# Context gates moved between the recurrence features, with twelve latent gates of the last layer beside them

## The chip, the cores and the metric

The kernel runs on one core of one Trainium2 chip. The metric is the device time in microseconds (us) from the first to the last instruction of the program on that core. TensorE (PE in the rows) does the matrix products into PSUM, VectorE (DVE) and ScalarE (ACT) do elementwise work, GpSimd (POOL) does elementwise work and gathers, and SyncE (SP) issues most DMAs. Each engine works through its own list of instructions in the order in which the program was built, so an instruction that waits also holds whatever stands behind it.

## The reference, cut to what matters

Two layers transform 512 latent and 256 context tokens of width 1024. In each layer one input projection feeds four token mixers and four vectors of gates:

```
p_lat = (x * (1 + sc1) + sh1) @ w_in[l]
p_ctx = (ctx * (1 + csc1) + csh1) @ w_in[l]
mla_lat, rwkv_lat, gqa_lat, win_lat, gate_lat = split_last(p_lat, GROUP_WIDTHS)
...
acc = gates[:, :, 0] * (ys[0] @ w_branch[0])      # gates = sigmoid(gate_pre), 4 x 1024 columns
```

The gates are needed only when the branches are merged, late in a layer. The context stream is not carried out of the last layer, so its context gates are never needed; its latent gates are. Gates are 4096 columns, made in 32 chunks of 128.

## The kernel before, in words

Every product with a weight is done in three passes to keep fp32 accuracy. `wload` and `wtile` fetch a weight chunk of 512 KB on SP's queue (`wr`), round it on ScalarE (`wH`, line 204), and subtract on VectorE or GpSimd to get the rest (`wL`, line 205, called a split below). TensorE then does, for each of eight slices of the inner dimension, high by high, high by low and low by high: 24 matmuls for a chunk, of 256 columns for the context tokens and 512 for the latent ones. Four pairs of buffers hold split weights in stage S1.

A layer goes through these stages:

- S1, features. `feature(f, m)` makes 15 chunks of the recurrence projection for all 768 tokens (48 matmuls each: 24 of 512, 24 of 256 columns). For each of four pairs of heads the order is `k`, `r`, `v`; after them `rates` (small products, line 349), `keys` (products `kksq`, line 360, on the normalised keys), `unit` (transposes `krep` and the scaling of `kkr`), and `prepare`, a long run on VectorE and ScalarE. `prepare` of one pair is done while TensorE makes the features of the next; its last result `ksum` feeds the product in `bonus` (line 430).
- S1, natural. `natural` makes three blocks of columns in token order (line 499), with two or three rounds of `ada_round` (modulation weights of 8 MB each) between them.
- S1, heads. `heads(0)` and `heads(1)` normalise, rotate, transpose and split queries and keys. `context` makes the 32 context gates in layer 0, sixteen behind each `heads`; in the last layer it makes none.
- S2. The recurrence for four pairs of heads, one after the other. For each pair VectorE inverts blocks by `eliminate` (lines 742 and 745), then twelve steps go from engine to engine. Thirty-two latent gates (`gate_lat`, split on GpSimd) have the lowest priority, and the scheduler puts their matmuls wherever it sees TensorE free.
- Then attention and merge, the output projection, and the experts.

The builder's scheduler sets the order of every engine from the order of the calls and its own view of what is ready. The names in rows: `pw` is a two-bank PSUM tile of S1 or S2, `pl` the PSUM tile of a latent gate or of an ada round, `pn` that of a natural block or of a small product, `X` the modulated input.

Of the kernel before, what the change touches and what calls it, by code (L numbers as in the profile page):

```python
# [8 lines left out]
F32 = mybir.dt.float32  # L9
# [47 lines left out]
STEPS = 3  # L57

# [20 lines left out]
def tile_backbone(ctx: ExitStack, tc: tile.TileContext, I, out, taps=None, upto=99):  # L79
# [89 lines left out]
    def mm_acc(outs, lhs, rhs, nk):  # L169
        """outs: list of (psum ap, lo, hi); lhs/rhs: functions k -> (H, L); moving sliced by lo:hi"""  # L170
# [13 lines left out]
    # ------------------------------------------------------------------ weight stream  # L184
# [26 lines left out]
    # ------------------------------------------------------------------ modulation  # L211
# [3 lines left out]
    def ada_round(l, r, ps, sb, ring=None, bufs=4):  # L215
        """columns r * 2048 .. of layer l: four groups of 512, one column tile of the array each"""
# [30 lines left out]
    def xtiles(l):  # L247
        """the modulated input of layer l in two parts, latent and context, on the other side of SBUF"""
# [7 lines left out]
    # ------------------------------------------------------------------ layers  # L256
    for l in range(DEPTH):
# [5 lines left out]
        with xlat:  # L263
            # ---------------------------------------------------------- S1 projections
            T3B = 12
            with xctx, ExitStack() as e1:
# [42 lines left out]
                # RWKV features, transposed  # L309
                with ExitStack() as er:  # L310
                    pr = er.enter_context(tp(name=f"pr{l}", bufs=1))
                    psw = er.enter_context(tp(name=f"s0w{l}", bufs=3, space=PSUM))
# [74 lines left out]
                    def prepare(hp, r, k, v, kk, rt):  # L387
                        """decayed queries and keys of a pair of heads, bonus"""
# [63 lines left out]
                    for hp in range(4):  # L452
                        r, k, v = [pr.tile([P, T], F32, name=nm(n), tag="rk", bufs=8) for n in "rkv"]
                        feature(4 + hp, k)
                        feature(hp, r)
                        rt = [rates(hp, 0)]
                        kk, pn = keys(hp, k)
                        for f in late:
                            f()
                        feature(8 + hp, v)  # L460
# [8 lines left out]
                    for f in late:  # L469
                        f()  # L470
                if upto < 2:
                    return
# [11 lines left out]
                # natural projections  # L484
# [22 lines left out]
                def rope(dst, x, b, nh, hd):  # L507
                    """dst, x: [P, nh, hd]"""
# [80 lines left out]
                # context gates  # L589
                def gate_chunk(f, lat, cx, pp, dst):  # L590
                    W = wload(I["w_gate"][l, f], [P, DC, P])
                    pw = pp.tile([P, 1024], F32, name="pw")
                    proj_t(pw, W, lat, cx)
                    lo, hi = (0 if lat else TL), (T if cx else TL)
                    ac.activation(dst[:, lo:hi], pw[:, lo:hi], AF.Tanh, scale=0.5)
                    ac.dma_start(gscr[f][:, lo:hi], dst[:, lo:hi])
# [1384 lines left out]
```

## Time and profile before

| what | us |
|---|---|
| median of three runs | 6534.53 |
| lowest and highest of them | 6518.1 and 6548.82 |
| span of the profiled execution (the page gives no other time for it) | 6533.5 |
| layer 0: features, natural, heads with gates, S2 | 217.0, 175.6, 146.1, 526.3 |
| layer 1: features, natural, heads, S2 | 210.0, 174.0, 37.9, 507.9 |

The stages are stretches of the span, cut where the first instruction of the next one starts on TensorE. The rest of the span is attention, the experts and the norms, which the change does not touch. The profile's page gives busy time per engine; a busy TensorE may still be working at half its clock, so the granted clock (PEclk, as a share of 2.4 GHz) is read beside it.

### The profile page before, as it was taken

What the parts mean: (1) busy time and instruction counts of PE and PEld (TensorE: products, weight loads), DVE (VectorE), ACT (ScalarE), POOL (GpSimd) and SP (SyncE); (2) the same over time, 40 slices, a digit from 0 to 9 for tenths busy, and PEclk for the clock granted to TensorE, in tenths of its full rate; (3) what the DMA queues carried; (4) which work ended last, traced back from release to release, by engine and by line L of the source; (5) the groups of instructions that cost most, each with busy time, mean ns of one, the idle gap of its engine ahead of it and who ended that gap; (6) DMA issues with size and microseconds to landing.
All of it is one profiled execution on the core that took longest, in us unless ns stands there. A gap on an engine that the chain in (4) does not pass through costs nothing.

```text
span 6533.5 us, 95628 instructions
## 1 busy us (share of the span) xinstructions
PE 5912.4 (90%) x35605; PEld 4895.5 (75%) x35605; DVE 4508.9 (69%) x9402; ACT 2371.0 (36%) x4585; POOL 2217.2 (34%) x1721
## 2 busy tenths in 40 slices
PE   8898998999897998889899788798999888999998
PEld 5677665778776886667677566666678788999998
DVE  6535554667698857888888674546456798578887
ACT  3223222444335842222222332222334467433333
POOL 1101222000038846656655211133100168444442
PEclk9998897999998999999999899799899999999999
DMA  4455222031435688888899435422121446888896
GB/s 175 157 192 181 84 85 72 11 87 58 148 109 185 229 280 305 303 305 315 316 334 335 171 107 177 131 93 74 68 64 41 156 148 226 291 292 294 296 331 246
DMA packets 532162, 1220.90 MB, mean 187 GB/s; under 512 B 46321, under 2 KB 249201, under 8 KB 524017
## 3 DMA queue, kind: packets, MB, share of 16 engines
q1 hardware_dynamic: 339728, 718.16, 33.2%
q0 software_dynamic: 111168, 406.63, 17.0%
q10 hardware_dynamic: 80800, 90.00, 4.0%
q8 instruction: 281, 4.60, 0.3%
q14 instruction: 185, 1.51, 0.1%
HBM read 1041.41 MB, written 173.21 MB: 186 GB/s over the span
## 4 chain that ended last, share of the span: by engine, by line
PE 48%; DVE 14%; issue 8%; DMA 8%; POOL 5%; ACT 2%; SPq 0%; ACTq 0%; POOLq 0%; DVEq 0%
PE pu L1538 10%; PE pa L1789 7%; PE po L1101 4%; POOL row L1008 3%; PE pl L176 3%; PE pm L176 3%; DMA row<-in_peer_v,gix 3%; PE pw L1070 3%; PE ptp L182 2%; PE pv L1789 2%; PE pn L499 2%; DMA row<-in_peer_v 2%; PE pg L1465 2%; DMA row<-in_peer_u,gix 2%; PE pw L176 1%
## 5 line engine op out<-in xcount | busy, mean ns | idle before, releaser
L1538 PE MATMUL pu<-HX,wH 128*128 128x512 f32 (+2 forms) x4608 | 1327.4, 371 | 11.5 <-ACT wH L1524 6.0
L1538 PEld LDWEIGHTS pu<-HX,wH 128*128 128x128 f32 x4608 | 855.9, 194 | 115.1 <-ACT ga L1777 7.0
L1538 PE MATMUL pu<-HX,wL 128*128 128x512 f32 (+2 forms) x2304 | 848.3, 368 | 41.6 <-POOL wL L1526 36.1
L1008 POOL DMA_INDIRECT row<-in_peer_u,gix x384 | 495.3, 1290 | 513.9 <-DVE row L1648 281.1
L1008 POOL DMA_INDIRECT row<-in_peer_v,gix x384 | 495.5, 1290 | 454.6 <-DVE accn L1657 237.9
L1630 ACT CAST wH<-row 128x1024 fp32r<-128x1024 f32 x384 | 401.9, 1047 | 609.2 <-DMA row<-in_peer_v 286.6
L1789 PE MATMUL pa<-CL,wH 128*128 128x512 f32 (+1 forms) x1536 | 566.5, 369 | 26.0 <-DVE CL L1769 25.8
L1789 PE MATMUL pa<-CH,wH 128*128 128x512 f32 (+1 forms) x1536 | 563.7, 367 | 21.5 <-ACT CH L1764 21.4
L1648 DVE SCALAR_TENSOR_TENSOR row<-row,hn 128x1024 f32<-128x1024 f32 x384 | 504.4, 1323 | 99.0 <-DMA row<-in_peer_u,gix 96.8
L1789 PE MATMUL pa<-CH,wL 128*128 128x512 f32 (+1 forms) x1536 | 562.3, 366 | 0.0
L1657 DVE SCALAR_TENSOR_TENSOR accn<-row,gcw,accn 128x1024 f32<-128x1024 f32 x381 | 519.3, 1374 | 61.4 <-DMA row<-in_peer_v,gix 60.8
L1646 DVE TENSOR_TENSOR wL<-row,wH 128x1024 fp32r<-128x1024 f32 x384 | 478.3, 1246 | 119.4 <-ACT wH L1630 118.6
L1538 PEld LDWEIGHTS pu<-HX,wL 128*128 128x128 f32 x2304 | 445.4, 193 | 100.9 <-POOL wL L1526 42.7
L204 ACT CAST wH<-wr 128x1024 fp32r<-128x1024 f32 (+1 forms) x222 | 231.0, 1043 | 574.9 <-PE pl L176 188.4
L980 POOL TENSOR_TENSOR lnst<-lnst,mhalf 128x4 f32<-128x4 f32 (+3 forms) x8 | 9.4, 1180 | 1183.1 <-DVE lnst L979 1183.1
L176 PE MATMUL pl<-X,wH 128*128 128x512 f32 x1024 | 403.7, 457 | 3.7 <-DVE qk L585 3.2
L205 POOL TENSOR_TENSOR wL<-wr,wH 128x1024 fp32r<-128x1024 f32 x64 | 214.4, 3355 | 545.4 <-ACT wH L204 278.2
L1449 POOL TENSOR_SCALAR B<-cst,T 128x128 f32<-128x128 f32 x330 | 383.4, 1170 | 33.6 <-PE pg L1465 20.7
L1789 PEld LDWEIGHTS pa<-CL,wH 128*128 128x128 f32 x1536 | 291.2, 190 | 72.2 <-DVE CL L1769 41.3
L1789 PEld LDWEIGHTS pa<-CH,wH 128*128 128x128 f32 x1536 | 291.2, 190 | 61.4 <-ACT CH L1764 29.1
L205 DVE TENSOR_TENSOR wL<-wr,wH 128x1024 fp32r<-128x1024 f32 (+1 forms) x158 | 191.3, 1213 | 189.3 <-ACT wH L204 188.1
L1764 ACT CAST CH<-ga 128x512 fp32r<-128x512 f32 (+1 forms) x256 | 145.0, 566 | 467.6 <-DVE ga L1761 349.3
(400 smaller groups left out, 13619.4 us busy)
## 6 DMA issues: line engine op xcount, KB each, us to landing
row<-in_peer_v SPq DMA_DIRECT2D x256, 512.0 KB
wr<-in_uT SPq DMA_DIRECT2D x128, 512.0 KB
row<-in_uT SPq DMA_DIRECT2D x128, 512.0 KB
wr<-in_ada_w SPq DMA_DIRECT2D x96, 512.0 KB
wr<-in_w_gate SPq DMA_DIRECT2D x96, 512.0 KB
gdr<-gall SPq DMA_DIRECT2D x32, 1024.0 KB
Gt<-gdr SPq DMA_DIRECT2D x32, 1024.0 KB
gdr<-big SPq DMA_DIRECT2D x24, 1024.0 KB
```

Source lines behind the costliest of these rows:

```text
L176: pe.matmul(o, lw, rw[:, lo:hi], start=(k == 0 and a == 0), stop=(k == nk - 1 and a == 2))
L204: ac.copy(H, raw)
L205: lsplit[0] = (split or ve).tensor_tensor(L, raw, H.bitcast(F32), op=OP.subtract)
L1008: gp.indirect_dma_start(out=rows, out_offset=None, in_=tab, in_offset=bass.IndirectOffsetOnAxis(ap=ix, axis=0))
L1101: pe.matmul(o[r0:r0 + 64, o0:o0 + P], vx(kb), pt[:, j * P:(j + 1) * P], start=(j == 0), stop=(j == nk - 1))
L1449: (gp if e == "gp" else ve).tensor_scalar(B[:, j, :], iota, T3[:, 1, t_ + j:t_ + j + 1], T3[:, 2, t_ + j:t_ + j + 1], op0=OP.is_equal, op1 ...
L1538: pe.matmul(pw[:, :hi - lo], w[:, k, :], x[:, k, :], start=(k == 0 and i == 0), stop=(k == DC - 1 and i == 2))
L1630: ac.copy(H, ready[nx[1]])
L1646: ve.tensor_tensor(L, raw, H.bitcast(F32), op=OP.subtract)
L1648: ve.scalar_tensor_tensor(raw, raw, 1.0, hn[y], op0=OP.mult, op1=OP.mult, accum_out=acts[y][:, j:j + 1])
L1657: ve.scalar_tensor_tensor(accn[y], raw, gcw[y][:, j:j + 1], accn[y], op0=OP.mult, op1=OP.add)
L1789: pe.matmul(pv[:, :TD], w[:, ds], x, start=(k == 0 and i == 0 and (fresh or s == 0)), stop=(k == 1 and i == 2 and (fresh or s == NS - 1)))
```

## The change

The context gates are made by a new function `gate_early` in the features stage, two behind each `k`, each `r` and each `rates`/`keys` block of the four pairs in layer 0 (24), and the remaining eight behind the last feature. In the last layer, which has no context gates, one latent gate is made at each of these twelve places, and `gate_lat` in S2 starts from number 12. `psw` of the features stage shrinks from three two-bank tiles to two, and the two banks go to a pool of two single tiles, `psg`. Nothing is computed differently. Docstrings and comments were dropped as well, which shifts line numbers.

```diff
+EARLYG = (32, 12)
...
+                def gate_early(f, pp):
+
+                    H, L = wload(I["w_gate"][l, f], [P, DC, P])
+                    lo, hi = (0, TL) if last else (TL, T)
+                    x = X[0 if last else 1]
+                    pw = pp.tile([P, 512], F32, name="pg")
+                    mm_acc([(pw[:, :hi - lo], 0, hi - lo)], lambda k: (H[:, k, :], L[:, k, :]),
+                           lambda k: (x[0][:, k, :], x[1][:, k, :]), DC)
+                    g = s1.tile([P, T], F32, name=nm("gate"), tag="t3", bufs=T3B)[:, :hi - lo]
+                    ac.activation(g, pw[:, :hi - lo], AF.Tanh, scale=0.5)
+                    ac.dma_start(gscr[f][:, lo:hi], g)
+
+                early = list(range(EARLYG[l]))
+
+                def gates(n, pp):
+                    for _ in range(min(n, len(early))):
+                        gate_early(early.pop(0), pp)
...
-                    psw = er.enter_context(tp(name=f"s0w{l}", bufs=3, space=PSUM))
+                    psw = er.enter_context(tp(name=f"s0w{l}", bufs=2, space=PSUM))
+                    psg = er.enter_context(tp(name=f"s0g{l}", bufs=2, space=PSUM))
...
                         feature(4 + hp, k)
+                        gates(2 - last, psg)
                         feature(hp, r)
+                        gates(2 - last, psg)
                         rt = [rates(hp, 0)]
                         kk, pn = keys(hp, k)
                         for f in late:
                             f()
+                        gates(2 - last, psg)
                         feature(8 + hp, v)
...
                     for f in late:
                         f()
+                    gates(len(early), psg)
...
                 heads(0, nats[1])
-                context(0, 16)
+                ada()
                 heads(1, nats[2])
-                context(16, 32)
+                ada()
...
-                for f in range(32):
+                for f in range(EARLYG[l] if last else 0, 32):
                     gate_lat(f)
```

TensorE, layer 0, between the second and the third pair of the features stage. `la` feeds the rates, `v` is transposed for the pair before, `kksq` is this pair's norm, `ksum` the bonus of the pair before. Before, these small products stand together ahead of the `v` feature, and `kksq` stands 27 matmuls into it:

```order
L349 MATMUL pw<-la,a_289 128x512
L349 MATMUL pw<-la,a_289 128x256
L182 MATMUL pw<-cst,v_433 128x128 x6
L430 MATMUL pw<-ksum_678,cst 128x512
L430 MATMUL pw<-ksum_678,cst 128x256
L302 MATMUL pw<-X_112,wH_915 128x512
L306 MATMUL pw<-X_114,wH_915 128x256
```

The same place in the change, where `pg` is the PSUM tile of an early gate:

```order
L177 MATMUL pg<-X_115,wH_1185 128x256
L177 MATMUL pg<-X_114,wL_1186 128x256
L369 MATMUL pw<-la,a_292 128x512
L369 MATMUL pw<-la,a_292 128x256
L183 MATMUL pw<-cst,v_436 128x128 x6
L177 MATMUL pg<-X_114,wH_1258 128x256
L380 MATMUL pn<-cst,kksq_1229 128x2 x6
L177 MATMUL pg<-X_115,wH_1258 128x256
L177 MATMUL pg<-X_114,wL_1259 128x256
```

Forty-eight gate matmuls now stand ahead of these products, `kksq` has moved ahead of the bonus and of the whole `v` feature, and 47 more gate matmuls stand around the bonus behind it. On VectorE the stretch from one pair's `krep` to the next pair's `kkr` holds two splits before and five in layer 0 (four in layer 1) now; three more stand in one row ahead of the next `krep`.

TensorE, layer 0, at `heads(1)`. Before, the twenty transposes of `xo` and ten of `nwin` have context gates on both sides (gate matmuls are L306 here):

```order
L306 MATMUL pw<-X_115,wH_4000 128x256
L306 MATMUL pw<-X_114,wL_4001 128x256
L182 MATMUL pw<-cst,xo_4032 128x128 x5
L182 MATMUL pw<-cst,xo_4045 128x128 x5
L182 MATMUL pw<-cst,xo_4064 128x128 x5
L182 MATMUL pw<-cst,xo_4083 128x128 x5
L182 MATMUL pw<-cst,nwin 128x128 x10
L306 MATMUL pw<-X_114,wH_4135 128x256
```

In the change the ada round (L225, `glat` its result) ends just ahead of them, and the first latent gate of S2 (`pl<-X`) follows:

```order
L225 MATMUL pl<-wr_4426,sc_104 32x512 x2
L183 MATMUL pl<-cst,glat_4430 128x128 x4
L183 MATMUL pw<-cst,xo_4580 128x128 x5
L183 MATMUL pw<-cst,xo_4593 128x128 x5
L183 MATMUL pw<-cst,xo_4612 128x128 x5
L183 MATMUL pw<-cst,xo_4631 128x128 x5
L183 MATMUL pw<-cst,nwin 128x128 x10
L177 MATMUL pl<-X_112,wH_8461 128x512
```

Nothing but transposes is left to TensorE between the end of the ada round and S2.

TensorE, layer 1, S2, the last recurrence step but one of the fourth pair. Before, it holds a gate matmul (L176) between the product of `S` with `AR` (L836) and that with `TT` (L844):

```order
L836 MATMUL pw_37608<-S_37601,AR_36343 64x64 x2
L836 MATMUL pw_37608<-S_37601,AR_36346 64x64 x2
L176 MATMUL pl<-X_30567,wL_38764 128x512
L807 MATMUL pw_37660<-S_37601,AR_36343 64x64
L844 MATMUL pc<-w0s_37613,TT 64x64 x4
```

The same step in the change:

```order
L843 MATMUL pw_37987<-S_37980,AR_36759 64x64 x2
L843 MATMUL pw_37987<-S_37980,AR_36762 64x64 x2
L814 MATMUL pw_38039<-S_37980,AR_36759 64x64
L851 MATMUL pc<-w0s_37992,TT 64x64 x4
L864 MATMUL pw_37987<-UV_36767,nat_37890 64x64 x2
```

The gate matmul is gone. Most steps hold four to seven gate matmuls before; in the change they still do in the first two pairs, while the third and fourth pair's steps, the whole inversion of the fourth pair, and that of the third pair behind its 77th gate matmul hold none. At the end of layer 1's features stage, 61 matmuls of the first natural block now stand ahead of the last bonus, where before all of them stood behind it; in layer 0 the 144 matmuls of six gates stand there instead, behind the bonus.

## Rows read from the trace of the kernel before

**Rows 1.** The page: busy time of each engine, share of the span, instructions.
```profile
PE 5912.4 (90%) x35605; PEld 4895.5 (75%) x35605; DVE 4508.9 (69%) x9402; ACT 2371.0 (36%) x4585; POOL 2217.2 (34%) x1721
```

**Rows 2.** Windows by stage; columns: stretch, length, busy time (instructions), PEclk, DMA share, GB/s.
```profile
35.00:252.00 217.00, 178.41 (x895) 141.88 (x896) 174.54 (x247) 77.89 (x113) 36.99 (x61) 0.89 0.37 126
427.60:573.70 146.10, 120.77 (x884) 103.34 (x880) 65.22 (x75) 50.23 (x75) 4.64 (x2) 0.92 0.75 240
3735.00:3945.00 210.00, 174.33 (x884) 139.38 (x884) 158.12 (x217) 69.80 (x97) 38.05 (x46) 0.88 0.34 114
4118.97:4156.90 37.93, 13.82 (x63) 10.38 (x61) 30.29 (x45) 8.31 (x12) 2.13 (x1) 0.59 0.72 209
4156.90:4664.80 507.90, 458.20 (x4012) 330.96 (x4012) 286.13 (x718) 131.25 (x285) 148.72 (x124) 0.88 0.28 90
```

**Rows 3.** Waits of TensorE, layer 0 features: total us, times, longest.
```profile
PE pw L430 <- DVE ksum L427: 20.2, 3, 16.8
PE pw L349 <- ACT buf L336: 6.1, 3, 2.2
```

**Rows 4.** Timeline of VectorE, layer 0 features: start, length, instruction, idle before.
```profile
131.76 1.23 DVE L205 TENSOR_TENSOR wL<-wr,wH 128x1024 fp32r<-128x1024 f32 x1 [4.27 <-ACT wH L204]
133.43 0.56 DVE L368 COPY krep<-kst 128x768 f32<-128x768 f32 x1
...
167.88 0.61 DVE L355 TENSOR_SCALAR kkr<-k,vec 128x768 f32<-128x768 f32 x1
...
177.90 0.56 DVE L368 COPY krep<-kst 128x768 f32<-128x768 f32 x1
```

**Rows 5.** Timeline of TensorE, layer 1 features; 93 feature matmuls stand between these two.
```profile
3827.80 0.82 PE L182 MATMUL pn<-cst,krep 128*128 128x128 f32 x6
...
3844.61 1.55 PE L349 MATMUL pw<-lw,w 64*128 64x512 f32 x4
```

**Rows 6.** Timeline of ScalarE: results of context gates; one more gate ends between them.
```profile
558.86 0.39 ACT L595 ACTIVATE gate<-pw 128x256 f32<-128x256 f32 x1 [0.40 <-ACT gate L595]
564.83 0.39 ACT L595 ACTIVATE gate<-pw 128x256 f32<-128x256 f32 x1 [0.40 <-ACT gate L595]
```

**Rows 7.** Timeline of ScalarE in S2, layer 1: results of two successive latent gates.
```profile
4435.43 0.59 ACT L911 ACTIVATE glat<-pl 128x512 f32<-128x512 f32 x1
4441.03 0.58 ACT L911 ACTIVATE glat<-pl 128x512 f32<-128x512 f32 x1
```

**Rows 8.** Window during layer 0's last ada round, columns as in rows 2.
```profile
440.00:460.00 20.00, 15.20 (x76) 7.42 (x76) 6.32 (x8) 3.58 (x5) 0.00 (x0) 0.92 1.08 364
```

**Rows 9.** Timeline of VectorE, layer 1: heads(1) begins.
```profile
4138.37 0.81 DVE L514 TENSOR_TENSOR rope<-nwin,cst 128x640 f32<-128x640 f32 x1
```

**Rows 10.** Timeline of TensorE, layer 1: first natural block, three matmuls apart.
```profile
3949.13 0.55 PE L499 MATMUL pn<-wH,X 128*128 128x416 f32 x2
...
3949.71 0.55 PE L499 MATMUL pn<-wH,X 128*128 128x416 f32 x2
```

**Rows 11.** Timeline of VectorE, layer 1, inversion of the last pair.
```profile
4570.53 0.48 DVE L742 TENSOR_TENSOR tmp<-W,X 128x150 f32<-128x150 f32 x2
4570.91 4.80 DVE L745 TENSOR_TENSOR X<-X,tmp 128x150 f32<-128x150 f32 x2
...
4582.60 2.29 DVE L742 TENSOR_TENSOR tmp<-W,X 128x50 f32<-128x50 f32 x1
```

**Rows 12.** Timeline of GpSimd in the same stretch.
```profile
4563.42 12.19 POOL L205 TENSOR_TENSOR wL<-wr,wH 128x1024 fp32r<-128x1024 f32 x2 [3.13 <-ACT wH L204]
```

**Rows 13.** Timeline of TensorE, one recurrence step of the third pair, layer 1.
```profile
4520.21 0.34 PE L836 MATMUL pw<-S,AR 64*64 64x64 f32 x8
...
4524.39 0.73 PE L176 MATMUL pl<-X,wH 128*128 128x512 f32 x2
4525.05 0.34 PE L836 MATMUL pw<-S,AR 64*64 64x64 f32 x8
```

**Rows 14.** Window at the start of layer 1's first recurrence.
```profile
4220.00:4240.00 20.00, 20.00 (x191) 15.26 (x191) 8.19 (x9) 6.04 (x12) 4.33 (x5) 0.50 0.02 4
```

More of the change, by code (lines that the diff above doesn't have):

```diff
@@ L587, in heads @@
                                 ac.dma_start(qkscr[br][i][:, :, (b - 1) * P:b * P], qk[i].bitcast(F32))
[L590 to L596, printed above, removed]
-                rounds = ROUNDS[l][:]
-                def context(a, b):
-                    for f in range(a, b):
-                        if not last:
-                            g = s1.tile([P, T], F32, name=nm("gate"), tag="t3", bufs=T3B)
-                            gate_chunk(f, False, True, psw, g)
-                        if f % 16 == 8:
-                            ada()
+                rounds = ROUNDS[l][:]
                 def ada():
```

## The prediction

> **What bounds the kernel now.** I read the page first: TensorE is busy for 90% of the span [rows 1], so work that only changes its place gains nothing; what counts is the time in which TensorE waits, at the place that work leaves and at the place to which it goes. Then I cut the span into the stages that the change touches [rows 2]. In layer 0's features TensorE is idle for 217.0 - 178.4 = 38.6 us, in layer 1's for 210.0 - 174.3 = 35.7, each time with VectorE busy for 75 to 80%. In layer 0's heads, with the 32 context gates, it is idle for 25.3. Layer 1's heads show what that stage is without gates: 37.9 us, of which VectorE works 30.3. S2 of layer 1, with 32 latent gates, takes 507.9 us at 458.2 of TensorE. Last I went into single places: the waits of TensorE in the features [rows 3], where the longest, 16.8 us, is the last bonus waiting for `ksum`, and the timelines of one pair.
>
> One pair of the features is a circle of 177.90 - 133.43 = 44.5 us from `krep` to `krep` [rows 4]. From `krep` to the end of the next `kkr` (167.88 + 0.61) are 35.1 us, in which VectorE has no gap; the other 9.4 are the norm, the rest of the `v` feature and small products. So VectorE sets the first stretch and TensorE the second, and a matmul is free only if it is put into the first.
>
> **The change part by part.** *The price of a gate.* Two context gates end 564.83 - 558.86 = 5.97 us apart [rows 6], so one is 3.0 us of TensorE, or 0.125 a matmul; 32 are 96. A latent gate takes 5.6 us [rows 7], 0.23 a matmul; twelve are 67. A split on VectorE takes 1.23 us [rows 4]. A feature matmul takes (3844.61 - 3828.62) / 93 = 0.172 us on the mean [rows 5].
>
> *Layer 0's heads, -106.* The 146.1 us lose their gates and become layer 1's bare stretch of 37.9 [rows 2]. The last ada round now has nothing to cover its loads: twelve loads of 0.52 MB, at the 364 GB/s of [rows 8], are 17 us, and behind it `heads(1)` takes 4156.9 - 4138.37 = 18.5 [rows 9]; together 36 to 38 if the loads run at that rate. I take 40. If they ran at half of it, the stage would be 55, so the gain lies between 91 and 108.
>
> *Layer 0's features, +81.* The first pair has TensorE as its limit and pays in full for its six gates: +18. In the three pairs after it the order puts into the first stretch two splits become five, so VectorE needs 35.1 + 3 x 1.23 = 38.8, less the bonus product (under 1 us) that left it: 38. TensorE's own work there is 95 feature matmuls (16.3), about 94 gate matmuls (11.8) and some 5 us of small products, 33 in all: covered. The second stretch gets 47 gate matmuls (5.9), the bonus (some 1.5) and the 27 matmuls of `v` (4.6) that stood ahead of `kksq`: 9.4 + 12.0 = 21.4. The circle is then 59.4 instead of 44.5, and three of them cost +45, where 54 were put in. At the end, 45 gate matmuls stand inside the 16.8 us of waiting and are free; the splits ahead of `ksum` and six gates behind the bonus cost +18. In all 81 of 96. If every idle microsecond were filled it would be 96 - 38 = 58, and if none were, 96.
>
> *Layer 1's features, +40.* The first pair pays three gates, +17. Then the first stretch has two splits more: 35.1 + 2.5, about 37.5, against 33 of TensorE. The second gets 23 latent gate matmuls (5.3) and the 27 of `v` (4.6): 19.3. The circle is 56.8 or, with the bonus product gone from the first stretch, 56.3, three times +11.8: +35. At the end the 61 natural matmuls that now stand ahead of the bonus take 0.193 us each [rows 10], so 11.8 of the last wait is filled: -12. Bounds as before: 31 to 67.
>
> *Layer 1's S2, -30.* Twelve gates leave, all from the third pair's inversion on. The inversion is VectorE's: while GpSimd makes two splits in 12.2 us [rows 12], two subtractions that take 0.48 together as the product ahead of them does cost 4.80; a single one costs 2.29 where its neighbours take 0.22 [rows 11]. So four splits cost the inversion 8.6 us, and the third pair loses one of its own, 2.1: 10.7. The Trainium skill, page SBUF — State Buffer, section "SBUF: two separate sides", says that VectorE and GpSimd hold a port pair for a whole instruction while the loser stands still; the trace agrees (4.80 for 0.48). The rule also speaks against the early splits, which read two operands on VectorE: in layer 0 they could hold GpSimd for 32 x 1.23 = 39 us more, beside 37.0 us of work in 217.0 [rows 2]; by the rule the sum would stay as it is unless `prepare` waits for GpSimd just then, and no row here prices that. Between inversion and recurrence 18 gate matmuls stood in each pair, mostly on the path: -6 for two pairs. A recurrence step takes 4.84 us and holds five or six gate matmuls [rows 13]; two of them stand between the outputs and the next `S` by `AR`, the rest in waits that remain. I take 0.6 us for each of 22 steps: -13. Bounds: 0 if the chain keeps its pace, -67 if TensorE alone set it.
>
> *The smaller pool of `pw`.* Two tiles instead of three make a small product wait for the copy two tiles back; one such wait of 2.2 us stands in every pair already [rows 3]. In layer 0 gate matmuls lie between, in layer 1 two or three only, inside the stretch that VectorE sets. Price nothing, up to 2 us a pair, 12 in all, if that cover is gone.
>
> *The sum.* -106 + 81 + 40 - 30 = -15 on a span of 6533.5. That span lies 1 us under the median of the three runs, so I forecast 6519 us, from 6495 to 6543 by itself (heads 15 worse; features and S2 10 to 15 either way).
>
> **The rivals.** *S2 gives the gates back in full.* If TensorE's queue alone set the pace of the third and fourth pair, S2 would fall by 67 instead of 30: 6482. For it speak 458 us busy of 508 [rows 2]; against it that the inversion is VectorE's.
>
> *VectorE stands at the splits (slower).* A split waits for ScalarE's cast, which waits for one of four buffers that TensorE must have freed; 4.27 us of it show in the pair of [rows 4], and everything of `prepare` is queued behind, then `ksum`, then TensorE's bonus. If each added split of the first stretch (three, and two in layer 1) waits that long, three pairs cost 38 and 26 us more: 6519 + 64 = 6583. It decides when these waits pass 15 us over the six pairs, 2.5 us a pair. Against it: the new order holds buffers for shorter chunks, so they come free sooner.
>
> *The clock.* With no gates beside it the fourth pair's inversion leaves TensorE nearly without work, and its recurrence then starts at 1.2 GHz, as layer 1's first one did, granted 0.50 behind an inversion [rows 14]. If the two bare recurrences ran at that level throughout, the 3.7 us of a step that are not gates would double, +2.6 in 16 steps with outputs, and the 13 gained are gone: 6519 + 41 + 13 = 6573. The Trainium skill, page TensorE: Matmul & The Clock Gate, section "HAM oscillation — how this bites in real kernels", says that a TensorE left waiting falls to half its clock again and again; the row agrees for a start, but no run here shows a whole recurrence without gates.
>
> *The idle only moves.* If the features fill nothing, +96 and +67 stand against -106 and -30: +27, 6562. For it speaks that TensorE's waits are for VectorE, which gets more to do; against it that those 16.8 us at the end are plainly open to work.
>
> **How the numbers follow.** Forecast 0.46; S2 in full 0.21; splits 0.15; clock 0.06; idle only moves 0.12. About half a percent, 33 us, is what a measurement of this kernel can tell. Faster than 6502: all of the second case and a fifth of the first, 0.30. Slower than 6567: two thirds of the splits, most of the clock, a few hundredths of the last, 0.17. Within: 0.53. The range leaves a tenth on either side: 6474 to 6577.
>
> **What would show it.** In the changed profile: layer 0 from the end of the natural blocks to S2's first gate near 40 us; a pair's circle near 59 us in layer 0 and 56 in layer 1, with a wait of TensorE at `kksq` of 4 to 6 us in place of those at `la` and `v`; the inversion of layer 1's fourth pair free of stretched subtractions; its steps near 4.2 us. I am wrong if the circle stays under 54 or passes 64, if layer 0's bare heads take over 50 us, or if bare steps take as long as before.

## The result, and the profile after

The changed kernel is slower: median 6581.42 us against 6534.53, ratio 1.0062 with a 95% interval of 1.0039 to 1.0084, or 41 us (25 to 55). The forecast was 6519, the range ended at 6577. The profiled execution has a span of 6586.8 us, 53.3 more than before.

The same stretches as in [rows 2], cut where the first TensorE instruction of the next stage starts; the natural blocks are shown too:

```profile
core 0: us, PE busy (x) PEld busy (x) DVE busy (x) ACT busy (x) POOL busy (x), PEclk, DMA share, GB/s
35.00:341.00 306.00, 274.01 (x1667) 237.24 (x1665) 212.05 (x278) 118.38 (x174) 45.60 (x61) 0.92 0.49 159
341.00:526.90 185.90, 174.17 (x1177) 141.51 (x1176) 48.50 (x107) 35.06 (x70) 16.70 (x4) 0.95 0.47 154
526.90:575.80 48.90, 28.29 (x116) 12.00 (x112) 30.31 (x46) 8.89 (x13) 0.26 (x1) 0.76 0.87 289
575.80:1118.60 542.80, 489.42 (x4250) 353.57 (x4250) 289.47 (x733) 135.38 (x300) 154.99 (x123) 0.87 0.28 86
3748.00:4015.00 267.00, 254.08 (x1234) 205.07 (x1234) 173.36 (x229) 87.56 (x121) 40.72 (x49) 0.95 0.38 125
4015.00:4182.80 167.80, 157.60 (x1100) 126.78 (x1099) 46.92 (x106) 33.04 (x68) 14.75 (x4) 0.99 0.48 159
4182.80:4220.80 38.00, 14.13 (x63) 10.52 (x61) 30.29 (x45) 8.31 (x12) 2.19 (x1) 0.56 0.73 208
4220.80:4716.80 496.00, 408.91 (x3724) 301.04 (x3724) 272.65 (x718) 112.64 (x261) 113.50 (x112) 0.74 0.23 73
```

Stage by stage, against the table of the profile before:

| stage | before | after | difference | forecast |
|---|---|---|---|---|
| layer 0, features | 217.0 | 306.0 | +89.0 | +81 |
| layer 0, natural | 175.6 | 185.9 | +10.3 | 0 |
| layer 0, heads | 146.1 | 48.9 | -97.2 | -106 |
| layer 0, S2 | 526.3 | 542.8 | +16.5 | 0 |
| layer 1, features and natural | 384.0 | 434.8 | +50.8 | +40 |
| layer 1, heads | 37.9 | 38.0 | 0 | 0 |
| layer 1, S2 | 507.9 | 496.0 | -11.9 | -30 |

The rest of the span is 4 us shorter. Of the 68 us between this span and the forecast's -15, layer 0's features and natural blocks have 18, its heads 9, its S2 16.5, layer 1's features and natural blocks 11 and its S2 18. Two lines stand out. The natural blocks and S2 of layer 0 grew although none of their work changed; and S2 of layer 1, which lost twelve gates of 5.6 us, gave back 11.9 us at a mean granted clock of 0.74 where it had 0.88.

Where it shows, first in VectorE's timeline of one pair in layer 0, the rows that answer to [rows 4]:

```profile
111.48 0.55 DVE L388 COPY krep<-kst 128x768 f32<-128x768 f32 x1
149.39 0.62 DVE L375 TENSOR_SCALAR kkr<-k,vec 128x768 f32<-128x768 f32 x1
170.28 0.56 DVE L388 COPY krep<-kst 128x768 f32<-128x768 f32 x1
```

The circle is 58.8 us, 38.5 to the end of `kkr` and 20.3 behind it. The forecast was 59.4, 38 and 21.4.

Then TensorE's timeline from layer 0's last bonus to the natural blocks:

```profile
317.37 2.90 PE L450 MATMUL pw<-ksum,cst 128*128 128x512 f32 x4 [14.06 <-DVE ksum L447]
...
340.00 1.04 PE L225 MATMUL pl<-wr,sc 128*32 128x512 f32 x2
340.97 0.65 PE L523 MATMUL pn<-wH,X 128*128 128x416 f32 x2
...
350.47 1.06 PE L523 MATMUL pn<-wH,X 128*128 128x416 f32 x2 [6.96 <-ACT wH L205]
```

The wait for `ksum` is still 14.06 us (16.8 in [rows 3]): most gates of the stage's end stand behind the bonus, not in the wait. Then come 20 us of gates, and then a new wait: a cast of `w_in` is late. In the timelines of ScalarE's and SP's queues and the DMA view of 326 to 352 us (busy share in tenths and rate in 40 slices of 0.65 us; an issue's KB and us to landing), what it waits for:

```profile
329.70 0.48 ACTq L505 DMA_DIRECT2D gains<-in_gqa_q_norm  x1
...
333.75 0.38 SPq L196 DMA_DIRECT2D wr<-in_w_in  x1
347.80 0.33 SPq L196 DMA_DIRECT2D wr<-in_ada_w  x1
```

```profile
DMA  9036999989997697612100000000012288899989
GB/s 361 21 36 95 353 388 414 359 239 348 364 363 259 184 260 228 225 75 72 40 23 20 13 22 20 23 19 12 21 30 82 101 247 326 308 243 296 338 276 397
...
gains<-in_gqa_q_norm ACTq DMA_DIRECT2D x1, 256.0 KB, 18.1
```

The load of `w_in` issued at 333.75 lands 15.7 us later, the longest of that tile's here; their median is 5.4. From 339.0 to 345.5, well inside its wait, the DMA moves only 12 to 30 GB/s: the gain vectors of the head norms are loaded in small packets (1526 of the packets in these 26 us are under 512 B), and take 18 us. The DMA engines' busy share is 0 or 1 tenth there, so they are not full either; why a load waits beside them no run shows. The kernel before loads these vectors at the same place, but had `w_in` in SBUF by then. The 7 us of waiting cost more than themselves, since TensorE then goes on at half its clock (window of the next 10 us, columns as above):

```profile
350.00:360.00 10.00, 8.20 (x20) 6.29 (x21) 2.05 (x2) 2.89 (x8) 0.00 (x0) 0.50 0.65 202
```

Last, windows of layer 1's third and fourth recurrence from the first to the last `w0s`, and two steps in VectorE's timeline of the fourth:

```profile
4544.50:4595.00 50.50, 43.56 (x366) 30.74 (x366) 12.26 (x47) 9.06 (x33) 7.72 (x18) 0.50 0.08 25
4658.20:4708.70 50.50, 43.63 (x366) 30.76 (x366) 12.34 (x46) 9.11 (x34) 7.72 (x18) 0.50 0.00 1
```

```profile
4681.02 0.29 DVE L846 TENSOR_TENSOR w0s<-pw,KV 128x128 f32<-128x128 f32 x1 [2.53 <-PE pw L843]
4686.82 0.29 DVE L846 TENSOR_TENSOR w0s<-pw,KV 128x128 f32<-128x128 f32 x1 [2.52 <-PE pw L843]
```

And the same two windows of the kernel before, not shown ahead:

```profile
4489.70:4535.50 45.80, 45.80 (x426) 29.93 (x426) 12.32 (x47) 13.46 (x39) 14.69 (x21) 0.98 0.26 79
4611.10:4656.70 45.60, 44.72 (x422) 29.25 (x422) 14.84 (x49) 13.74 (x40) 10.91 (x19) 0.98 0.15 49
```

With 60 and 56 matmuls fewer, both recurrences take 5 us more. The granted clock is 0.50 from end to end, 1.2 GHz, and TensorE is busy for 86% of the stretch with the step's own small matmuls. The step shown, one with outputs, takes 5.80 us, where [rows 13] has 4.84 with its gate matmuls in it.

### The profile page after: what moved, and what is told of

It reads as the page before. It is cut to its first block, busy times and chain, and to the rows that moved or that the text cites. A ratio compares the mean times of both kernels' runs of the same rounds, so it can differ in the third digit from the quotient of the medians.

```text
span 6586.8 us, 95630 instructions
## 1 busy us (share of the span) xinstructions
PE 5947.9 (90%) x35605; PEld 4929.4 (75%) x35605; DVE 4505.0 (68%) x9414; ACT 2369.7 (36%) x4585; POOL 2195.9 (33%) x1709
## 5 line engine op out<-in xcount | busy, mean ns | idle before, releaser
L1796 PE MATMUL pa<-CH,wH 128*128 128x512 f32 (+1 forms) x1536 | 565.5, 368 | 22.2 <-ACT CH L1771 22.2
L206 DVE TENSOR_TENSOR wL<-wr,wH 128x1024 fp32r<-128x1024 f32 (+1 forms) x170 | 205.8, 1213 | 235.9 <-ACT wH L205 234.4
L177 PE MATMUL pl<-X,wH 128*128 128x512 f32 x832 | 331.4, 461 | 6.1 <-DVE qk L609 6.1
L1796 PEld LDWEIGHTS pa<-CH,wL 128*128 128x128 f32 x1536 | 292.6, 191 | 31.0
```

The costliest lines, as they stand in the source:

```text
L177: pe.matmul(o, lw, rw[:, lo:hi], start=(k == 0 and a == 0), stop=(k == nk - 1 and a == 2))
L206: lsplit[0] = (split or ve).tensor_tensor(L, raw, H.bitcast(F32), op=OP.subtract)
L1796: pe.matmul(pv[:, :TD], w[:, ds], x, start=(k == 0 and i == 0 and (fresh or s == 0)), stop=(k == 1 and i == 2 and (fresh or s == NS - 1)))
```

## The experiments

**Which layer loses it.** Two kernels make one layer's move alone. Each is the changed kernel with one number of its table at zero, and the layer whose gates stay keeps three tiles of `pw`. Where layer 0's gates stay, they are back in the heads, behind the ada rounds.

```diff
-EARLYG = (32, 12)
+EARLYG = (32, 0)     # layer 0 alone
+EARLYG = (0, 12)     # layer 1 alone
...
```

> Only layer 0's 32 context gates move; layer 1's latent gates stay in S2. Theory: in the profile of the changed kernel layer 0's features and natural blocks grew by 99 us and its heads shrank by 97, so the move is worth nothing by itself, and the 17 us that its S2 lost besides, all in one recurrence at granted 0.50, are the clock's and need not come again: 6536 us, up to 6553 if that recurrence is slow here too. Rival (my forecast was right for layer 0 and layer 1 lost it all): 6534 - 25 = 6509.

> Only layer 1's twelve latent gates move; layer 0's context gates stay in its heads. Theory: layer 1's features and natural blocks lose 51 us, its S2 gives back 12, since its last two recurrences run at 1.2 GHz with steps of 5.05 us: 6534 + 39 = 6573. Rival (the forecast for layer 1, +40 and -30, was right and layer 0 lost it all): 6544.

Layer 0 alone: 6544.76 us, ratio 1.0014 (0.9991 to 1.0036), 9 us over the kernel before, the interval from -6 to +24. Its circles are 58.2 us, and all four recurrences of its layer 0 run at granted 1.00. Layer 1 alone: 6571.7 us, ratio 1.0043 (1.0027 to 1.0060), 28 us over (18 to 39). Its circles are 56.4 to 57.9, its last two recurrences 50.4 and 50.5 us at granted 0.50. So the forecast of -25 for layer 0 is outside its interval, and so is +10 for layer 1; the theory's +2 and +39 are inside, the second at the edge. Both layers missed.

**The smaller pool.** The kernel before, with one number changed:

```diff
-psw = er.enter_context(tp(name=f"s0w{l}", bufs=3, space=PSUM))
+psw = er.enter_context(tp(name=f"s0w{l}", bufs=2, space=PSUM))
```

> No gate moves; only the pool of pw in the features has two tiles instead of three. Theory: the third tile was never needed, circles stay at 44.5 and 43.5 us: 6534. Rival (two tiles make every pair wait): up to 2 us a pair, 16 in all, 6550, and the circles 46 us.

```profile
144.33 0.56 DVE L368 COPY krep<-kst 128x768 f32<-128x768 f32 x1
192.03 0.55 DVE L368 COPY krep<-kst 128x768 f32<-128x768 f32 x1
```

These two rows of VectorE's timeline are 47.7 us apart, 3.2 more than in [rows 4]; layer 1's circles are 47.2 to 47.8 instead of 43.6 to 44.5. So the rival holds for the circles, and with more than its 2 us a pair: in layer 0's three circles TensorE waits 23.6 us, six times, for the copies that empty `pw`. The time, 6551.62 us, ratio 1.0013 (0.9997 to 1.0030), fits both: the natural blocks catch up with part of it.

**Is it in the changed kernel's circles?** Two kernels give `pw` its third tile again while layer 0's gates come early (layer 1's don't). In one the gates take their turn in that pool; the other starts from the kernel with eight gates back in the heads (below) and leaves one bank each to the gates and the norm.

```diff
 # share3
-gates(2 - last, psg)
+gates(2 - last, psw)     # psw: bufs=3, no psg
 # banks311
-psw bufs=2, psg bufs=2, psn bufs=2
+psw bufs=3, psg bufs=1, psn bufs=1
```

> Layer 0's 32 gates early, layer 1's not, and no PSUM banks of their own: the early gates take their turn in the pool of pw, which has its three tiles again. Theory: two tiles alone made a circle 47.7 us instead of 44.5, 3.2 more, and the same 3.2 are in the 58.2 of layer 0 alone: circles of 55 us, the kernel 10 to 13 us under layer 0 alone, 6533. Rival (with gates between the features the small products no longer wait for the third tile): circles stay at 58, 6545.

> Layer 0 alone with eight gates back in the heads; in the features the pool of pw has three tiles again, and the early gates and the norm's sums one bank each instead of two. Theory (the 3.2 us a circle that two tiles of pw cost without gates are in the 58.2 too): circles 55 us, the kernel 10 to 13 us under 6522. Rival (they are hidden under the gates, and a single bank makes a gate wait for the tanh of the one before): circles 58 us or more, 6522 or more.

In neither is the circle shorter. With the shared pool the circles are 61.0 to 61.5 us (ratio 1.0031, 1.0013 to 1.0048), longer even than the rival had it. With one bank each they are 58.9 to 60.3 (6519.83 us, ratio 0.9983, 0.9968 to 0.9998). Each of the two takes banks from something else, so neither is a clean test of the third tile. What bears on it more directly is TensorE's waits in the changed kernel's three circles: none is for a copy that empties `pw`, and nearly all, 12.7 us, are for the `tanh` of a gate. So the forecast's price of nothing fits this kernel, by its stated cover.

**Who sets the first stretch.** Layer 0 alone, the early gates' splits on GpSimd:

```diff
-H, L = wload(I["w_gate"][l, f], [P, DC, P])
+wn[0] += 1
+H, L = wtile(I["w_gate"][l, f], [P, DC, P], (wp, w1)[wn[0] % 2], split=gp)
```

> Layer 0's 32 gates early, layer 1's not, and the splits of the early gates on GpSimd instead of VectorE (2.4 us each there, 1.23 on VectorE). Theory (VectorE sets the first stretch, so three added splits are in the circle): first stretch 34.5 to 35 us instead of 38.1, circle 54.5 to 55, the kernel 11 us under layer 0 alone, 6534. Rival (GpSimd's splits make VectorE's two-operand work wait, as they did in the inversion, and prepare's own GpSimd work stands behind them): first stretch 40 us or more, circle over 60, 6550 or more.

The groups of VectorE's work in one first stretch, by form, with busy time and mean ns of one; layer 0 alone and then this kernel:

```profile
L363 DVE SCALAR_TENSOR_TENSOR mixt<-buf,vec,mixt 128x770 f32<-128x770 f32 x3 | 3.1, 1017 | 0.0
L432 DVE SCALAR_TENSOR_TENSOR b<-ta,kkr 128x768 f32<-128x768 f32 x2 | 1.9, 955 | 0.0
```

```profile
L433 DVE SCALAR_TENSOR_TENSOR b<-ta,kkr 128x768 f32<-128x768 f32 x2 | 5.7, 2856 | 0.0
L364 DVE SCALAR_TENSOR_TENSOR mixt<-buf,vec,mixt 128x770 f32<-128x770 f32 x3 | 5.2, 1726 | 0.0
```

The rival: the first stretch is 42.6 to 42.7 us instead of 38.1, the circle 62.8 to 63.9; 6558.09 us, ratio 1.0026 (1.0006 to 1.0046). VectorE has one split in the stretch instead of five and is busy just as long (37.4 and 37.6 us), since two-operand work beside GpSimd's splits takes up to three times as long (2.86 us for 0.96; in the other two stretches of layer 0 alone the mean of these `b` rows is 1.78 already). The Trainium skill, page SBUF — State Buffer, section "SBUF: two separate sides", says that the two engines hold a shared port pair for a whole instruction; these rows agree. And it waits 4.6 us for `pcm`. The splits belong on VectorE here, though it sets the stretch.

**The natural blocks' start.** Layer 0 alone with 24 early gates, the eight of the stage's end back in the heads:

```diff
 for f in late:
     f()
-gates(len(early), psg)
```

> Layer 0 alone with 24 gates early and the eight of the stage's end back in the heads, layer 1's latent gates not early. Theory: the 10 us that the natural blocks lost at their start (loads of w_in and ada_w share two raw buffers and stood behind the eight gates) do not come, nor the 22 us between ksum and the first natural matmul; eight gates cost the heads 24 us, of which up to 10 hide the loads of the last ada round: the first inversion of S2 begins at 582 to 592 us instead of 595, the kernel 3 to 13 us under layer 0 alone, 6532 to 6542. Rival (the natural blocks wait for the loads of w_in whoever is in front): their first copies still come 30 us or more behind ksum, and the kernel is 10 us over layer 0 alone.

TensorE's timeline behind the last `ksum`:

```profile
311.13 2.90 PE L454 MATMUL pw<-ksum,cst 128*128 128x512 f32 x4 [5.14 <-DVE ksum L451]
313.46 0.91 PE L527 MATMUL pn<-wH,X 128*128 128x416 f32 x1
```

The theory, in its numbers: natural matmuls follow the bonus at once, some stand ahead of it already (the wait for `ksum` is 5.14 us instead of 14.1), no wait for `w_in` is left, and S2's first inversion begins at 585.1. 6522.16 us, ratio 0.9980 (0.9959 to 1.0000): 22 us under layer 0 alone by the medians, where 3 to 13 were expected (that inversion comes 10 us earlier), and level with the kernel before or a little under it. The eight gates cost the heads 102.4 - 76.7 = 25.7 us from the last natural copy to that inversion, 3.2 each: on balance they hide nothing of the ada round there. Whether `w_in` is late for the buffers, as that expectation says, or for the gain vectors, this kernel cannot tell, since its loads come ahead of both.

Three more kernels tell it. Each loads the two vectors once, 64 KB in all, in the features' second pair and copies them on ScalarE to their ten places: the changed kernel, the one with 24 early gates in layer 0 alone, and the kernel before.

```diff
+if hp == 1:      # in the features; gain1: [P, 2, 64]
+    ac.copy(gain1.rearrange("p a b -> p (a b)"), k[:, 0:P])     # keeps the loads here
+    for i, n in enumerate(("gqa_q_norm", "gqa_k_norm")):
+        ac.dma_start(gain1[:, i, :], ...)
 # natural blocks
-    ac.dma_start(gains[:, o_:o_ + cntr, :], ...)
+    ac.copy(gains[:, o_:o_ + cntr, :], gain1[:, i:i + 1, :].to_broadcast([P, cntr, 64]))
```

> The changed kernel with the two gain vectors of the head norms loaded once each (64 KB in all) in the second pair of the features and copied on ScalarE to the ten places; before, 320 KB came in small packets at the natural blocks' start. Theory: these loads hold the DMA (12 to 30 GB/s in layer 0 while a load of w_in issued at 333.75 takes 15.7 us to land; the same stretch lies in front of layer 1's ada_w), so the 8.3 us of TensorE's wait for w_in in layer 0 and 6 of the 9.2 for ada_w in layer 1 go: 14 us under the changed kernel, 6567, and the load of w_in lands in 5 us or so. Rival (the natural blocks wait since their raw buffers come free late, behind the eight gates, whatever else is loaded): the waits stay within 2 us of 8.3 and 9.2, and the time is that of the changed kernel, 6581.

> Layer 0 alone with the eight gates back in the heads, and the gain vectors loaded as in its sibling. Theory: its natural blocks have no wait for w_in left, but the ada rounds in them wait for loads behind the gain vectors, 3 us in layer 0 and 3.2 in layer 1: 6 us under 6522, or 6516, ratio 0.997. Rival (what these loads held up was hidden): 6522.

> The kernel before with the gain vectors loaded as in its siblings, no gate moved. Theory: TensorE's waits for ada_w in the natural blocks, 3.5 us in layer 0 and 3.2 in layer 1, go, nothing else: 6 us under the kernel before, ratio 0.999. If it is as fast as its sibling with 24 early gates, the early gates are worth nothing in any form that was tried.

The waits of TensorE in the first of them from 312 to 525 us, layer 0's end of the features, its natural blocks (up to 512.8) and the start of its heads (us in total, times, longest):

```profile
PE pw L451 <- DVE ksum L448: 14.1, 1, 14.1
PE pl L225 <- DMA wr<-in_ada_w: 7.0, 2, 4.7
PE pg L177 <- ACT gate L319: 1.3, 1, 1.3
```

No wait for `w_in` is left, and its loads land in 4.0 to 4.7 us by the median; of the 7.0 us for `ada_w`, 2.3 lie in the natural blocks (2.4 in the changed kernel). The theory holds: from `ksum` to the last natural copy layer 0 takes 195.5 us instead of 209.0, 13.5 less where the waits were 8.3, since the stretch at half clock behind them is gone too (granted 1.00 from 341 to 440 us), and from the last `krep` to that copy layer 1 takes 190.2 instead of 197.9 (its wait for `ada_w` falls from 9.2 to 4.6). 6549.51 us, ratio 1.0028 (1.0012 to 1.0043), 22 us under the changed kernel by the ratios where 14 were expected; the two profiles show 13.5 + 7.7 = 21.

With 24 early gates in layer 0 alone it is 6505.92 us, ratio 0.9962 (0.9947 to 0.9977): 12 us less than without this edit, where 6 were expected, and 25 us under the kernel before (15 to 35; five runs). The intervals with and without the edit overlap; in the profiles layer 0's stretch from the last `krep` to the last natural copy is 5 us shorter (193.7 for 198.9) and layer 1's the same (202). The kernel before itself shows no gain from the earlier loads: 6525.02 us, ratio 1.0000 (0.9981 to 1.0019), an interval that holds the expected 0.999 too; but its waits for `ada_w` did not go (4.4 us in either layer's natural blocks). So 24 gates in layer 0's features are worth some 25 us, once nothing stands in the way of the stage behind them: layer 0's first recurrence begins at 631.4 us, in the kernel before with the same loads at 653.9.

**Where in a pair.** From layer 0 alone with 24 early gates (6522.16 us, gain vectors as in the kernel before), the third gate slot (behind rates and keys) emptied into the other two, and once with four gates put ahead of the last bonus as well:

```diff
 feature(4 + hp, k)
-gates(2, psg)
+gates(3, psg)
 feature(hp, r)
-gates(2, psg)
+gates(3, psg)
...
-gates(2, psg)
 feature(8 + hp, v)
...
+gates(4, psg)     # the second kernel only
 for f in late:
     f()
```

> Layer 0 alone, eight gates back in the heads as before, and the 24 early ones stand three behind k and three behind r of each pair; none stands behind rates and keys, in the stretch that TensorE sets. Theory: the second stretch loses two gates' matmuls (20.2 to 14.3 us), the first gains two splits (38.1 to 40.5), under which TensorE's own work (33 us and 5.9) still fits: circles 54.8 us instead of 58.2, the kernel 10 us under 6522, or 6512. Rival (the first stretch is full): it grows by what the second loses, circles stay at 58, 6522.

> As the kernel with three gates behind k and three behind r, and four of the eight gates from the heads at the features' end, ahead of the last bonus, in the 14 us in which TensorE waits for ksum. Theory: four splits make ksum 4.9 us later, the heads are 12.3 shorter: 7 us under its sibling, 6505. Rival (the gates' loads and splits hold back prepare or the natural blocks' first loads, as the eight did): the first natural copies come over 15 us behind ksum, and it is level with its sibling or slower, 6512 to 6520.

Rivals both times. With 3, 3, 0 the second stretch falls to 17.1 to 19.1 us, not 14.3, and the first grows to 40.9 to 42.1: circles of 59.1 to 60.5 and 6526.21 us, ratio 0.9983 (0.9966 to 1.0001). With four at the end `ksum` is 4.2 us later, where 4.9 were priced, but the first natural copy comes 20.2 us behind it: 6533.45 us, ratio 0.9996 (0.9981 to 1.0010), slower even than the rival's 6520. Neither place is shown to be cheaper than the ones the change took.

**The clock of the bare recurrences.** First the gates' place is filled again, with work that nothing uses; H and L are those of the last gate that stayed. Each product has its `tanh` behind it, as a gate's has.

```diff
 for f in range(EARLYG[l] if last else 0, 32):
-    gate_lat(f)
+    H, L = gate_lat(f)
+if last:
+    for _ in range(EARLYG[l]):
+        pw = psl.tile([P, 512], F32, name="pl")
+        mm_acc([(pw[:, :TL], 0, TL)], lambda k: (H[:, k, :], L[:, k, :]), ..., DC)
+        ...
```

> The changed kernel, and in layer 1's S2, where the twelve gates were, as many matmuls on the operands of the last gate that stayed: no load, no cast, no split, and what they make is used by nothing. TensorE gets work that the changed kernel had just been rid of. Theory (the bare recurrences ran at granted 0.50 since TensorE had too little to do): the granted clock of the last two recurrences comes back to 1.00, their steps to 4.6 us from 5.05, the fourth inversion stays near 23 us since no split disturbs it: 10 us faster than the changed kernel, or 6571. Rival (the bare steps are set by the chain through VectorE and ScalarE, whatever TensorE's clock): steps stay at 5.05 or grow, and the kernel is 0 to 15 us slower than the changed one, 6581 to 6596.

Windows of its last two recurrences:

```profile
4551.70:4596.50 44.80, 44.76 (x422) 28.90 (x422) 12.31 (x46) 10.95 (x37) 7.69 (x18) 1.00 0.09 28
4661.10:4705.90 44.80, 44.77 (x422) 28.94 (x422) 12.30 (x46) 10.36 (x36) 7.70 (x18) 1.00 0.01 1
```

With 56 matmuls more in each, they are 5.7 us shorter, at granted 1.00, 4.48 us a step on the mean of all ten (5.05 bare); the fourth inversion stays at 23.0. Of these 11 us the other added matmuls take 6 back, on the path between inversion and recurrence (19.3 us become 22.4 and 22.2); from layer 1's first `kkr` to the last step it is 911.3 us against 917.0. The median does not show that: 6590.37 us, ratio 1.0078 (1.0054 to 1.0102), its interval overlapping that of the changed kernel. So the clock and the steps went as the theory has it; the 10 us of the whole kernel it did not give.

That the bare ones are slow is no chance of one execution. Three kernels leave the third and fourth recurrence of layer 1 bare (the changed one, layer 1 alone, and the changed one with the vectors loaded early), and in their profiles these take 50.4 to 50.5 us six times out of six. In the twelve kernels that have gates or filling all along them, 22 of 24 take 44.8 to 46.5 us, and two 53.7.

Then only the first four steps of each are filled:

```diff
+if last and hp > 1 and s < 4:
+    for k in range(12):
+        pe.matmul(pa[:, 640:1024], XLH[:, k % DC, 0:P], XLH[:, k % DC, 0:384], ...)
 late = (s, S)
```

> The changed kernel, with twelve matmuls of 384 columns that nothing uses added to each of the first four steps of layer 1's third and fourth recurrence; the steps behind them are bare. What it tells: whether bare steps stay at granted 1.00 once the engine has been brought there. Theory A (bare steps have too little for the clock wherever they start): the granted clock is 1.00 in the steps with added matmuls or just behind them and back at 0.50 before the recurrence ends, whose last steps take 5.05 us. Theory B (only the bare start holds the clock down): 1.00 to the end, and the bare steps behind take 4.2 to 4.5 us, as forecast.

Windows of the fourth recurrence: the filled steps, the next 6 us, and the rest.

```profile
4652.90:4669.00 16.10, 11.91 (x106) 9.86 (x107) 3.26 (x12) 3.16 (x11) 2.56 (x6) 0.92 0.01 2
4669.00:4675.00 6.00, 4.99 (x52) 3.53 (x51) 1.35 (x5) 0.78 (x3) 0.85 (x2) 0.78 0.01 3
4675.00:4708.20 33.20, 30.31 (x246) 21.84 (x246) 7.70 (x29) 4.79 (x18) 4.27 (x10) 0.50 0.00 1
```

Theory A: once the added matmuls are over, the granted clock falls to 0.50 and stays there, and the bare steps take up to 5.82 us again, in the third recurrence as in the fourth. With the filled steps the two recurrences take 56.6 and 55.4 us, more than without. It is not the start that holds the clock down; these steps cannot keep it up. (One run, 6587.26 us.)

## Why the prediction was wrong

The step that failed most plainly is this one, of S2: "I take 0.6 us for each of 22 steps: -13." The two recurrences take 9.6 us more, not 13 less. The gain was worked out at the clock that the steps with gates had. At the lower one the first three steps, without outputs, take 11.7 and 11.8 us instead of 11.0 and 11.1, and the seven with outputs 38.7 instead of 34.8 and 34.5, or 5.5 each instead of 5.0: TensorE's own matmuls at 1.2 GHz take most of the step. This was the rival of the clock, at a chance of 0.06 and 6573 us. Its row, granted 0.50 at the start of a recurrence [rows 14], was the right one, and its condition came true; its price, 2.6 us a step, was more than four times too high. What was missed is that the recurrences of before, granted 0.91 to 1.00 as wholes, have gate matmuls in most of their steps, so none of them tells what a bare one gets. The Trainium skill, page TensorE: Matmul & The Clock Gate, section "HAM oscillation — how this bites in real kernels", tells of an engine that falls to half its clock while it waits; here it is there while busy for 86% of the stretch, so waiting alone does not account for it, and the measurement decides.

The rest of S2 came near what was priced: the fourth inversion is 23.0 us instead of 31.6, which is the 8.6 of four splits; between inversion and recurrence 23.3 and 24.6 us became 19.3 each, 9.3 instead of 6. The third inversion did not get shorter by 2.1 (33.5 for 32.5). Some 6 of the 11.9 us that S2 gave back lie ahead of all these, at its start and in the first recurrence, whose gates did not move: no term of the forecast has them. Of these, 2.5 are a first step of 4.4 us for 6.9, which is 6.9 again in the changed kernel with the vectors early: luck.

Layer 0's features: the circles are 58.8, 58.5 and 58.3 us for 59.4, so both stretches were read rightly. The wait of 4 to 6 us at `kksq` is not there; one of 4.3 stands at a gate instead, for the `tanh` that empties its bank. (In layer 1 there is one at `kksq`, of 2.6 us.) The first pair cost 22.7 for 18. The step that failed is the end, "the splits ahead of `ksum` and six gates behind the bonus cost +18": from the last `krep` to the end of the natural blocks it is 239.8 us for 204.8, so 35. `ksum` is 3 us later, the six gates with their start at a lower clock take 20, and the natural blocks take 10 more: 8.3 are two waits for `w_in`, and behind them TensorE runs at granted 0.50. The loads of `w_in`, held back behind the eight gates', meet those of the gain vectors. The forecast looked at the engines at this end and not at the queue of loads of the next stage. Either cure works: with the eight gates away, or with the vectors loaded early, the wait is gone.

Layer 0's heads: -97.2 for -106, inside the bounds and under the 50 us named. The term that was mis-sized is the 17 us of loads: the last products of the ada round end 31.5 us into the stage. From 526.9 to 560 us the queue of the weights moved 6.8 MB, and that of ScalarE's issues, mostly stores of queries and keys, 4.3 MB beside it, which the forecast left out. The waits are for the ada round, 10.9 us in all:

```profile
PE pl L225 <- DMA wr<-in_ada_w: 10.9, 5, 4.8
```

Layer 1's features: the first pair cost 17.0 for 17; the circles 56.4, 57.9 and 57.6 for 56.3 (from 43.6 to 44.5, where the forecast took layer 0's 44.5 for all three), so +40 for +35; and the end gave 6 instead of 12. The wait for `ksum` did fall, from 16.8 to 5.2 us, but TensorE then waits 9.2 us for `ada_w` in the natural blocks instead of 3.2: matmuls that come earlier meet loads that don't, behind the same gain vectors. With these out of the way the end gives 13.7 (203.9 us became 190.2), a little over the 12 forecast.

The forecast had no term for layer 0's S2, and needs none: of its 16.5 us one recurrence has 16.4, at a granted clock that the same instructions have in some kernels' profiles and not in others' (below). Without them, layer 0 makes +2 for -25, and layer 1 +39 for +10.

VectorE at the splits, the rival that gave 6583, has the right number by luck and the wrong cause: its added waits were to be in the circles, and those are as forecast, or 1 us over it in layer 1. That the idle only moves (6562) is nearer to what happened, except that the time was lost to the loads and to the clock, not to VectorE.

## What to carry to other kernels

Work that fills the gaps of a latency-bound chain may be what holds TensorE's clock: before moving it, look for the granted clock of that chain without the filler, and price the chain's own matmuls at that level. Where work is put at a stage's end, read the next stage's first loads too, with what else is in the DMA queues then: a slow small load that was hidden can become the path. The gates themselves were priced well, 3.0 us where they stood and (58.2 - 44.5) / 6 = 2.3 in a circle, which pays where nothing is lost behind them (ratio 0.9962, against 1.0000 for the kernel before with the same loads).

## What was not expected of the hardware

TensorE busy for 30.3 of 33.2 us with matmuls of 64 columns, and six of 128, is granted 0.50 throughout. With 56 matmuls of 512 columns among them in 44.8 us it is granted 1.00, and the stretch is shorter.

The recurrences that do have gates don't always get the clock at once. Layer 0's second one, the same instructions in the changed kernel, its two filled versions and layer 0 alone, took these times (windows of the changed kernel's first 50 us, and of the kernel with four filled steps):

```profile
789.00:839.50 50.50, 50.50 (x328) 33.03 (x332) 8.58 (x32) 12.20 (x36) 10.65 (x16) 0.61 0.22 65
```

```profile
793.30:844.50 51.20, 51.20 (x481) 34.16 (x481) 13.50 (x51) 14.90 (x44) 14.68 (x21) 1.00 0.31 96
```

In all, 66.9, 66.8, 51.2 and 51.2 us, in the order named. Others lose the clock on the way: layer 1's second recurrence in layer 0 alone takes 55.6 us for 45.7, and its last steps, with gates in them and TensorE busy throughout, run at half:

```profile
4373.50:4398.90 25.40, 25.40 (x147) 15.45 (x139) 4.90 (x18) 2.32 (x5) 4.05 (x5) 0.50 0.10 32
```

In the kernel before with the smaller pool it is layer 0's first (57.9 us for 51.1). What decides it no run here shows, so filling a chain made the full clock likely here and not certain.

Loads of 320 KB in small packets took 18 us, and for 6.5 of them the DMA moved 12 to 30 GB/s at a busy share of 0 or 1 tenth. A 416 KB load issued 4 us behind them took 15.7 us to land; the median of the loads of its tile in these 26 us is 5.4.
